# An all-engine loop moved half a stage earlier between the experts of a mixture, with new numbers for the ring of weights

## The chip, the cores and the metric

The kernel runs on one core of a Trainium2 chip. The metric is device time in microseconds (us). Before the change the median of three runs is 1884.03 us (1882.94 to 1884.06).

## The reference, cut to what matters

Two layers work on 512 tokens of width 1024 in float32. Each layer mixes tokens (attention and a convolution side by side, merged by two gates), then sends every token to 2 of 32 experts, then adds gated embeddings:

```python
for i in range(DEPTH):                                   # DEPTH = 2
    ...                                                  # h = norm(x); y_a: attention, y_b: convolution
    merged = sigmoid(ga) * y_a + sigmoid(gb) * y_b
    x = x + merged @ w_out[i]
    x = x + hier_moe(rms_norm(x), ...)                   # 32 experts, top 2
    g_ple = sigmoid(rms_norm(x) @ w_ple_gate[i])
    x = x + g_ple * (p[i] @ w_ple_proj[i])

hb = silu(xb @ w_gate[e]) * (xb @ w_up[e])               # one expert on its tokens
yb = hb @ w_down[e]
```

Every expert has its gate, up and down weights, 2 MB each, and all of them are read from memory once per layer. An expert that gets more tokens than a fixed capacity (64) must still serve them all.

## The kernel before, in words

**Mixing.** TensorE multiplies in three passes with numbers split in a high and a low half: each chunk of weights (a `raw` buffer of 512 KB, loaded at L207) is turned into `hi` by ScalarE (ACT, L225) and `lo` by GpSimd (POOL, L230); `s_hi` is read by the matmuls of L289 and L290, `s_lo` by those of L291. After the gates comes the merge, a loop over eight column blocks j = 0..7 with one chunk each (`ao0` to `ao7`). Block j has 12 matmuls into `ps_yb` and 12 into `ps_ya`. Then ScalarE adds a bias (L735), VectorE (DVE) applies the gates and adds (L736 to L738), and two halves of the result are split again: ScalarE writes `s_mTh` (L741), VectorE `s_mTl` (L742). The output product (`wo`) and the routing follow.

**Experts.** The 32 experts are 16 pairs, two pairs at a time: eight double pairs, c = 0..7. A double pair c runs gate and up products for both pairs (`ps_g`, `ps_u`, twice 32 matmuls each), then the third (down) products of double pair c - 1 (`ps_y`, 64 matmuls), transposes (`ps_hT`), the gather of the tokens for c + 1 (`ps_xg`) and the combination of double pair c - 1 into the tokens (`ps_c`). At c = 5 and 6 the embeddings' products (`ps_pe`) stand at the end; what they need is loaded at the start of c = 4 by `load_embeddings`: one tile `pT` (L1110), split by ScalarE and GpSimd, and two chunks at L207.

**Weights.** A double pair uses 48 pieces of 512 KB, 8 for each gate, up or down matrix of a pair. SyncE's queue (SP) issues them in the order of use, at L241 in `pump`, into `s4`, a pool of 45 buffers that serves many other tiles too. `pump(limit, keep)` stops when `limit` pieces are held, or when fewer than `keep` buffers would stay free. `RING` holds the limits in the mixing, one for each of three stretches; `KEEP` the reserved buffers for each c. After the routing's last steps `pump(keep=3)` is called with its default limit, 99; the last four pieces of double pair 0 come in halves (L253).

**The loop.** `overflow(l)` (L1218, L1219) handles crowded experts: a loop over as many extra blocks as the routing found. Its count is known only on the chip. With these inputs it is zero in both layers: no instruction of its body is in the trace. It is bracketed by barriers on which every engine waits, for all the others and for all transfers issued ahead of it. Before the change it stands behind the combination of c = `OVC` = 4.

**What sets the order.** The order on TensorE is the order of the code. On the other engines a scheduler sets it from the code and its own estimates. SP holds 8 transfers in flight; a piece's issue waits for the one 8 places ahead and for its buffer.

Of the kernel before, what the change touches and what calls it, by code (L numbers as in the profile page):

```python
# [53 lines left out]
              + [f"wo{i}" for i in range(8)] + ["pe0", "pe1"] + [f"pg{i}" for i in range(8)])  # L54
NCH = len(SEQ_CHUNKS)

RING = 6, 18, 28
KEEP = 6, 10, 6, 6, 8, 10, 12, 8
LAGS = 1, 2, 1, 5
OVC = 4  # L60
PEC = 5
PGD = "pg1", "pg2", "pg3"
PGS = 1, 3, 4, 5, 7
# [92 lines left out]
class Trunk:  # L156
# [310 lines left out]
    def mixer(self, l):  # L467
# [256 lines left out]
        for j in range(8):  # L724
# [20 lines left out]
            self.s4.free()  # L745
            self.pump(RING[0] + j)
        for s in oT + tuple(cv):
            s.free()
        self.pump(RING[1])


        pacc = [self.ps.get(F32, "wo") for _ in range(NT)]
        for i in range(4):
            self.step_b(pos[f"wo{i}"], pacc, mT, 2 * i, i == 0, i == 3)
            self.pump(RING[1])
        for t in range(NT):
# [10 lines left out]
        def hook():  # L767
            self.advance(steps)
            self.pump(RING[2], keep=3)
        for t in range(NT):  # L770
# [194 lines left out]
    def moe(self, l):  # L965
# [6 lines left out]
        def make_rows():  # L972
            for q in self.slots + list(self.gates) + [self.rc]:
                ps = self.ps.get(F32, "row")
                for t in range(NT):
                    pe.transpose(ps[:, t * P:(t + 1) * P], q[:, t:t + 1].to_broadcast([P, P]), self.ident)
                r_ = self.s2.get(F32, "row")
                act.activation(r_, ps, AF.Copy)
                self.ps.free()
                rows.append(r_)  # L980
# [23 lines left out]
        def scatter_hot(p):  # L1004

            col = self.cc(C_SLOT + p, 1)
            tmp = self.s2.get(F32, "oh")
            ga = self.tn(3, "ga", bufs=2)
            g_, rh[p] = self.tn(1, f"gs{p % 2}", bufs=2), self.tn(1, f"rs{p % 2}", bufs=2)
            v.tensor_scalar(tmp, rows[0], col, None, op0=OP.is_equal)  # L1010
            o = self.s2.get(F32R, "OHT")
            v.scalar_tensor_tensor(o, rows[1], col, tmp, op0=OP.is_equal, op1=OP.add)
            v.scalar_tensor_tensor(tmp, o.bitcast(F32), 0.5, rows[4], op0=OP.mult, op1=OP.mult, accum_out=rh[p])
            for i in range(2):
                v.scalar_tensor_tensor(tmp, rows[i], col, rows[2 + i], op0=OP.is_equal, op1=OP.mult,
                                       accum_out=ga[:, i:i + 1])
            v.tensor_scalar(g_, ga[:, 0:1], ga[:, 1:2], 2.0, op0=OP.add, op1=OP.mult)
            v.tensor_scalar(g_, g_, rh[p], rh[p], op0=OP.mult, op1=OP.mult)
            oht[p], gs[p] = o, g_
            self.s2.free()  # L1020

        def gate_up(p, xg, w, ps, hs):
            for h in hs:
                for k in range(2):
                    for e in range(2):
                        s = (2 * h + k) % 4 * GS + (2 * p % 4 + e) * CAP
                        pe.matmul(ps[64 * e:64 * e + 64], xg[h // 2][:, s:s + CAP], self.half_item((l, w, 2 * p + e, h), k),
                                  start=h == 0 and k == 0, stop=h == 3 and k == 1)
                for e in range(2):
                    self.item_free((l, w, 2 * p + e, h))  # L1030
                self.pump(keep=KEEP[self.c])

        def hidden(p, pg, pu):
            t = self.s2.get(F32, "h")
            act.activation(t, pg, AF.Tanh, scale=rh[p])  # L1035
            v.scalar_tensor_tensor(t, t, 1.0, pg, op0=OP.add, op1=OP.mult)  # L1036
            v.tensor_mul(t, t, pu)
            self.ps.free(2)
            return t

        def transp(p, t):
            ps = self.ps.get(F32, "hT")
            for f in range(4):
                pe.transpose(ps[:, f * P:(f + 1) * P], t[:, f * P:(f + 1) * P], self.ident)
            o = self.s2.get(F32, "hT")
            act.activation(o, ps, AF.Copy)  # L1046
            self.ps.free()
            self.s2.free()
            hT[p] = o

        def down(p):
            h_ = hT.pop(p)
            ps = [self.ps.get(F32, "y") for _ in range(2)]
            for f in range(4):
                for n in range(2):
                    for e in range(2):
                        pe.matmul(ps[n][64 * e:64 * e + 64], h_[:, f * P + e * CAP:f * P + (e + 1) * CAP],
                                  self.item_tile[l, "d", 2 * p + e, f][:, n * T:(n + 1) * T], start=f == 0, stop=f == 3)
                for e in range(2):
                    self.item_free((l, "d", 2 * p + e, f))  # L1060
                self.pump(keep=KEEP[self.c])
            self.s2.free()
            yh, yl = self.s4.get(F32R, "yh"), self.s4.get(F32R, "yl")
            for n in range(2):
                a = slice(n * T, (n + 1) * T)
                self.last = act.activation(yh[:, a], ps[n], AF.Copy, scale=gs[p]).ins
                v.scalar_tensor_tensor(yl[:, a], ps[n], gs[p], yh[:, a].bitcast(F32), op0=OP.mult, op1=OP.subtract)
            self.ps.free(2)
            ys[p] = (yh, yl)

        def combine(pl, then=None):
            for t in range(NT):
                for n in range(2):
                    ps = self.ps.get(F32, "c")
                    for i, p in enumerate(pl):
                        for o in range(2):
                            pe.matmul(ps, oht[p][:, t * P:(t + 1) * P], ys[p][o][:, n * T:(n + 1) * T],
                                      start=i == 0 and o == 0, stop=i == len(pl) - 1 and o == 1)
                    xs = self.x[t][:, n * T:(n + 1) * T]
                    v.tensor_add(xs, xs, ps)  # L1080
                    self.ps.free()
                if t == NT - 1:
                    self.s4.free(2 * len(pl))
                    self.s2.free(len(pl))
                if then:
                    then(t)

        def restore():

            self.x = [self.s4.get(F32, "x") for _ in range(NT)]  # L1090
            for x_, hi, lo in zip(self.x, *self.nh):
                nc.gpsimd.tensor_tensor(x_, hi.bitcast(F32), lo.bitcast(F32), op=OP.add)
# [14 lines left out]
        def load_embeddings():  # L1107
            self.pT = Rows(self.s4, 2, F32R, "pTh"), Rows(self.s4, 2, F32R, "pTl")
            praw = self.s4.get(F32, "pT")
            nc.sync.dma_start(praw, self.dr["pT"][l])  # L1110
            act.activation(self.pT[0].t[0], praw, AF.Copy)
            nc.gpsimd.tensor_tensor(self.pT[1].t[0], praw, self.pT[0].t[0].bitcast(F32), op=OP.subtract)
            self.s4.free()
            self.lim = self.pos["pe1"]
            self.look = self.ahead = 1
            self.load_chunks(self.lim)
            self.pp = []
# [9 lines left out]
        for c in range(NC2):  # L1127
            self.c = c
            prs = 2 * c, 2 * c + 1
            if c == PEC - 1:  # L1130
                load_embeddings()
            if c < NC2 - 1:
                oh = self.onehots(c + 1)
            ts = []
            for p in prs:
                pg, pu = self.ps.get(F32, "g"), self.ps.get(F32, "u")
                gate_up(p, xg, "g", pg, range(4))
                gate_up(p, xg, "u", pu, range(4))
                if p == 0:
                    with self.tc.issue_after(self.last_v), self.tc.issue_after(self.last_a):  # L1140
                        self.route()
                        make_rows()
                scatter_hot(p)
                ts.append(hidden(p, pg, pu))
            self.s4.free(2)
            if c == 1:
                restore()
            if c:
                for p in prs:
                    down(p - 2)  # L1150
            for p, t in zip(prs, ts):
                transp(p, t)
            if c < NC2 - 1:
                xg = [self.s4.get(F32, "xg") for _ in range(2)]
                for h in range(4):
                    gather(oh, xg, h)
                self.s4.free()
                if c == NC2 - 2:
                    self.s4.free(2 * NT)
            if c:  # L1160
                combine((2 * c - 2, 2 * c - 1))
            if c == OVC:
                self.overflow(l)
            if c in (PEC, PEC + 1):
                embeddings(c - PEC)
        self.lim = self.pos["pg7"]
# [317 lines left out]
```

## Time and profile before

| | |
|---|---|
| median of three runs | 1884.03 us |
| the profiled execution, whole | 1876.28 us |
| its span | 1874.5 us |
| TensorE busy | 1790.9 us (96%) |
| VectorE, ScalarE, GpSimd busy | 49%, 30%, 20% |
| transfers of the weights' queue | 477.04 MB, 66.9% of 16 engines' span |
| mean granted clock of TensorE | 0.989 |

The profiled execution lies 7.75 us below the median of the runs. TensorE sets the time; a change counts by what it adds to or takes from the time between two of its instructions. Busy time alone does not show a loss: a matmul that waits for its weights inside the pipeline can count as busy, so the prediction goes by starts.

### The profile page before, as it was taken

To read this page: it belongs to the slowest core of one execution; us is meant where nothing else is said; L and a number is where in the kernel's file an instruction comes from. 1 tells how busy PE (TensorE), PEld (TensorE's weight loads), DVE (VectorE), ACT (ScalarE), POOL (GpSimd) and SP (SyncE) were. 2 spreads that over 40 slices of the span, in tenths; PEclk is the share of its full clock that TensorE was granted. 3 is DMA by queue.
4 is the path that set the end of the run, shared out by engine and by line. 5 is a ranking of instruction groups with operands and counts; after the bars stand their busy time and mean duration, and the time that the engine had idled before them with its cause. 6 is when DMAs were issued, how large, how long until landed. Compare 5 with 4: busy or idle time off the path is not lost.

```text
span 1874.5 us, 23312 instructions
## 1 busy us (share of the span) xinstructions
PE 1790.9 (96%) x8532; PEld 1104.1 (59%) x8532; DVE 913.6 (49%) x2165; ACT 562.4 (30%) x1071; POOL 378.1 (20%) x201
## 2 busy tenths in 40 slices
PE   5999999999999989999989999999999999899987
PEld 4777777754555245454777767777545553455356
DVE  5587855463442243223657777536524432343146
ACT  4355443321111012113534445343211111021045
POOL 3445332401000001001444443242010000010021
PEclk9999999999999999999999999999999999999999
DMA  5212136389999899997231112554899999999951
GB/s 221 83 64 68 56 92 242 119 311 391 387 409 409 346 370 401 410 408 315 96 114 62 56 57 68 179 192 152 324 389 390 409 389 364 370 409 409 409 227 45
DMA packets 133319, 478.59 MB, mean 255 GB/s; under 512 B 14800, under 2 KB 15312, under 8 KB 133200
## 3 DMA queue, kind: packets, MB, share of 16 engines
q1 hardware_dynamic: 133200, 477.04, 66.9%
q8 instruction: 70, 1.15, 0.2%
q14 instruction: 49, 0.40, 0.1%
HBM read 474.89 MB, written 2.10 MB: 254 GB/s over the span
## 4 chain that ended last, share of the span: by engine, by line
PE 74%; DMA 10%; DVE 7%; issue 5%; ACT 2%; POOL 1%; SPq 0%; DVEq 0%; POOLq 0%; ACTq 0%
PE ps_g L94 11%; PE ps_u L94 10%; PE ps_y L94 9%; PE ps_z L290 5%; PE ps_z L289 5%; PE ps_z L291 5%; PE ps_xg L94 5%; PE ps_c L94 5%; DMA s_w<-wdn 4%; DMA s_w<-wg 3%; DMA s_w<-wu 2%; PE ps_tb L289 2%; PE ps_tb L290 2%; PE ps_tb L291 2%; PE ps_S L609 2%
## 5 line engine op out<-in xcount | busy, mean ns | idle before, releaser
L230 POOL TENSOR_TENSOR s_lo<-s_raw,s_hi 128x1024 fp32r<-128x1024 f32 x114 | 272.4, 2400 | 915.8 <-ACT s_hi L225 610.7
L94 PE MATMUL ps_g<-s_w,s_xg 128*64 128x512 f32 x1024 | 229.9, 602 | 11.2 <-DMA s_w<-wg 11.2
L94 PE MATMUL ps_y<-s_w,s_hT 128*64 128x512 f32 x1024 | 236.1, 595 | 3.5 <-DMA s_w<-wdn 2.9
L94 PE MATMUL ps_u<-s_w,s_xg 128*64 128x512 f32 x1024 | 231.2, 593 | 5.1 <-DMA s_w<-wu 4.9
L290 PE MATMUL ps_z<-s_hTl,s_hi 128*128 128x512 f32 x512 | 203.8, 398 | 0.0
L289 PE MATMUL ps_z<-s_hTh,s_hi 128*128 128x512 f32 x512 | 201.3, 393 | 0.0
L291 PE MATMUL ps_z<-s_hTh,s_lo 128*128 128x512 f32 x512 | 199.7, 390 | 0.0
L94 PEld LDWEIGHTS ps_y<-s_w,s_hT 128*64 128x64 f32 x1024 | 75.4, 137 | 159.9 <-issue 130.8
L94 PEld LDWEIGHTS ps_u<-s_w,s_xg 128*64 128x64 f32 x1024 | 74.0, 137 | 157.2 <-issue 141.1
L94 PEld LDWEIGHTS ps_g<-s_w,s_xg 128*64 128x64 f32 x1024 | 72.7, 139 | 155.4 <-issue 150.3
L501 DVE SCALAR_TENSOR_TENSOR s_acc<-ps_z,smt,s_acc 128x511 f32<-128x511 f32 (+27 forms) x210 | 153.8, 732 | 4.2
L1080 DVE TENSOR_TENSOR s_x<-s_x,ps_c 128x512 f32<-128x512 f32 x128 | 86.9, 688 | 89.4 <-PE ps_c L94 60.0
L225 ACT ACTIVATE s_hi<-s_raw 128x1024 fp32r<-128x1024 f32 x120 | 125.9, 1058 | 8.8 <-DMA s_raw<-wd 4.5
L94 PE MATMUL ps_xg<-s_OH,s_xh 128*128 128x256 f32 x476 | 117.4, 288 | 3.8 <-DVE s_OH L950 1.9
L1035 ACT ACTIVATE s_h<-ps_g,rs 128x512 f32<-128x512 f32 x32 | 22.0, 689 | 319.3 <-PE ps_g L94 286.5
L1046 ACT ACTIVATE s_hT<-ps_hT 128x512 f32<-128x512 f32 x32 | 17.7, 598 | 328.1 <-PE ps_hT L94 287.1
L94 PE MATMUL ps_xg<-s_OH,s_xl 128*128 128x256 f32 x476 | 115.9, 285 | 0.0
L290 PEld LDWEIGHTS ps_z<-s_hTl,s_hi 128*128 128x128 f32 x512 | 96.3, 188 | 21.2 <-issue 3.0
L289 PEld LDWEIGHTS ps_z<-s_hTh,s_hi 128*128 128x128 f32 x512 | 96.1, 188 | 21.3 <-issue 1.0
L1036 DVE SCALAR_TENSOR_TENSOR s_h<-s_h,ps_g 128x512 f32<-128x512 f32 x32 | 22.0, 688 | 177.5 <-ACT s_h L1035 177.5
L291 PEld LDWEIGHTS ps_z<-s_hTh,s_lo 128*128 128x128 f32 x512 | 96.3, 188 | 18.9
L94 PEld LDWEIGHTS ps_xg<-s_OH,s_xh 128*128 128x128 f32 x476 | 92.2, 194 | 5.7 <-issue 5.7
(256 smaller groups left out, 2852.4 us busy)
## 6 DMA issues: line engine op xcount, KB each, us to landing
s_w<-wu SPq DMA_DIRECT2D x256, 512.0 KB, 10.2
s_w<-wdn SPq DMA_DIRECT2D x256, 512.0 KB, 10.2
s_w<-wg SPq DMA_DIRECT2D x248, 512.0 KB, 10.2
s_raw<-wd SPq DMA_DIRECT2D x124, 512.0 KB, 3.5
s_w<-wg SPq DMA_DIRECT2D x16, 256.0 KB, 7.5
s_x<-x SPq DMA_DIRECT2D x4, 512.0 KB, 9.7
out<-s_n SPq DMA_DIRECT2D x8, 256.0 KB, 2.0
s_gain<-gains SPq DMA_DIRECT2D x3, 512.0 KB, 3.6
```

Of the source, the lines that this page charges most:

```text
L94: i = f(*a, **k)
L225: nc.scalar.activation(hi, raw, AF.Copy)
L230: nc.gpsimd.tensor_tensor(lo, raw, hi.bitcast(F32), op=OP.subtract)
L289: mm(out, lh, rh, start=start, stop=False)
L290: mm(out, lh, rl, start=False, stop=False)
L291: mm(out, ll, rh, start=False, stop=stop)
L501: v.scalar_tensor_tensor(o, i, w, o, op0=OP.mult, op1=OP.add)
L609: nc.tensor.matmul(ps[:, off:off + n], qk(0, i * P, (i + 1) * P)[r], qk(1, 0, n)[r], start=True, stop=True)
L1035: act.activation(t, pg, AF.Tanh, scale=rh[p])
L1036: v.scalar_tensor_tensor(t, t, 1.0, pg, op0=OP.add, op1=OP.mult)
L1046: act.activation(o, ps, AF.Copy)
L1080: v.tensor_add(xs, xs, ps)
```

## The change

The loop moves from the end of double pair 4 to double pair 3, directly behind the third products, ahead of the transposes, the gather and the combination. The limits of the ring in the mixing rise, and fewer buffers are reserved in most double pairs.

```diff
-RING = 6, 18, 28
-KEEP = 6, 10, 6, 6, 8, 10, 12, 8
+RING = 10, 21, 34
+KEEP = 2, 5, 5, 9, 5, 5, 5, 2
 LAGS = 1, 2, 1, 5
-OVC = 4
+OVC = 3
...
             if c:
                 for p in prs:
                     down(p - 2)
+            if c == OVC:
+                self.overflow(l)
             for p, t in zip(prs, ts):
                 transp(p, t)
...
             if c:
                 combine((2 * c - 2, 2 * c - 1))
-            if c == OVC:
-                self.overflow(l)
```

On TensorE in layer 0 the loop's instructions stand, before, behind the last combination of double pair 4 and ahead of the first gate product of double pair 5 (`s_OHT` is the table that scatters results back to tokens):

```order
L94 MATMUL ps_c_5204<-s_yl_5029,s_OHT_4498 128x512
L94 MATMUL ps_c_5204<-s_yh_5064,s_OHT_4580 128x512
L94 MATMUL ps_c_5204<-s_yl_5065,s_OHT_4580 128x512
L1218 TENSOR_LOAD nov
L1219 COMPARE_AND_BRANCH
L1219 UNCONDITIONAL_BRANCH x2
```

After the change, behind the last third product of double pair 3:

```order
L94 MATMUL ps_y_4630<-s_w_4543,s_hT_4284 64x512
L94 MATMUL ps_y_4630<-s_w_4549,s_hT_4284 64x512
L1218 TENSOR_LOAD nov
L1219 COMPARE_AND_BRANCH
L1219 UNCONDITIONAL_BRANCH x2
```

The transposes `ps_hT`, the gather `ps_xg` and the combination `ps_c` of double pair 3 now stand behind the loop.

On SP before, in layer 0, the loop has 238 issues of L241 ahead of it, the last two of them gate pieces (`s_w` from `wg`):

```order
L241 DMA s_w_5052<-wu 128x1024
L241 DMA s_w_5054<-wu 128x1024
L241 DMA s_w_5060<-wg 128x1024
L241 DMA s_w_5062<-wg 128x1024
L1219 COMPARE_AND_BRANCH
L1219 UNCONDITIONAL_BRANCH x2
```

After the change 193, the last five of them gate pieces, and the embeddings' loads come directly behind the loop:

```order
L241 DMA s_w_4639<-wu 128x1024
L241 DMA s_w_4641<-wg 128x1024
L241 DMA s_w_4647<-wg 128x1024
L241 DMA s_w_4649<-wg 128x1024
L241 DMA s_w_4655<-wg 128x1024
L241 DMA s_w_4657<-wg 128x1024
L1219 COMPARE_AND_BRANCH
L1219 UNCONDITIONAL_BRANCH x2
L1110 DMA s_pT_5053<-pT 128x1024
L207 DMA s_raw_5057<-wd 128x1024
L207 DMA s_raw_5059<-wd 128x1024
L241 DMA s_w_5084<-wg 128x1024
```

The loop stands 45 pieces earlier in SP's list. In both versions 34 issues of L241 stand ahead of those of L253, at the start of the experts.

On ScalarE in the merge of layer 0, before, the split of the chunk for block 4 (`s_hi_2362`) stands ahead of the two halves of block 3's result (`s_mTh`, from `ps_ya_2368`):

```order
L735 ACTIVATE ps_yb_2369<-ps_yb_2369,smt 128x512
L225 ACTIVATE s_hi_2362<-s_raw_2206 128x1024
L741 ACTIVATE s_mTh_2234<-ps_ya_2368 128x256
L225 ACTIVATE s_hi_2404<-s_raw_2324 128x1024
L741 ACTIVATE s_mTh_2236<-ps_ya_2368 128x256
L735 ACTIVATE ps_yb_2411<-ps_yb_2411,smt 128x512
```

After the change the same split (`s_hi_2370`) stands behind both halves (from `ps_ya_2376`):

```order
L735 ACTIVATE ps_yb_2377<-ps_yb_2377,smt 128x512
L741 ACTIVATE s_mTh_2234<-ps_ya_2376 128x256
L741 ACTIVATE s_mTh_2236<-ps_ya_2376 128x256
L225 ACTIVATE s_hi_2370<-s_raw_2206 128x1024
L225 ACTIVATE s_hi_2412<-s_raw_2332 128x1024
L735 ACTIVATE ps_yb_2419<-ps_yb_2419,smt 128x512
```

Each ScalarE instruction starts behind the one above it, so the split of block 4's weights now comes behind work on block 3's finished sums. The same exchange is there in layer 1.

## Rows read from the trace of the kernel before

**Rows 1.** Chain that ended last, layer 0: start, us, what
```profile
551.35 7.02 PE ps_g L94 x32
...
578.97 13.73 PE ps_y L94 x64
...
608.67 7.02 PE ps_g L94 x32
...
744.91 5.44 PE ps_pe L94 x24
750.35 7.02 PE ps_g L94 x32
```

**Rows 2.** Chain that ended last, layer 1
```profile
1505.32 13.73 PE ps_y L94 x64
...
1676.39 7.02 PE ps_g L94 x32
```

**Rows 3.** TensorE's timeline at the loop, layers 0 and 1: start, us, line [idle before <-releaser]
```profile
683.84 8.60 PE L94 MATMUL ps_g<-s_w,s_xg 128*64 128x512 f32 x32 [5.57 <-DMA s_w<-wg]
...
1610.71 9.37 PE L94 MATMUL ps_g<-s_w,s_xg 128*64 128x512 f32 x32 [5.65 <-DMA s_w<-wg]
```

**Rows 4.** Chain that ended last, around the loop, layer 0
```profile
673.16 10.09 DMA s_w<-wg
...
683.27 0.03 SPq L1219
```

**Rows 5.** SP's queue, layer 0
```profile
598.94 9.26 SPq L241 DMA_DIRECT2D s_w<-wg  x8
609.14 0.33 SPq L1110 DMA_DIRECT2D s_pT<-pT  x1
...
623.73 4.99 SPq L241 DMA_DIRECT2D s_w<-wu  x8
630.51 19.96 SPq L241 DMA_DIRECT2D s_w<-wdn  x16
651.43 9.29 SPq L241 DMA_DIRECT2D s_w<-wg  x8
661.67 9.25 SPq L241 DMA_DIRECT2D s_w<-wu  x8
671.89 14.80 SPq L241 DMA_DIRECT2D s_w<-wg  x8
```

**Rows 6.** SP's queue, layer 1
```profile
1525.30 9.30 SPq L241 DMA_DIRECT2D s_w<-wg  x8
```

**Rows 7.** Windows: us, busy us of each engine, granted clock, DMA share, GB/s
```profile
392.00:394.00 2.00, 0.30 (x2) 0.33 (x3) 1.97 (x18) 0.00 (x0) 0.00 (x0) 1.00 1.05 382
684.00:686.00 2.00, 2.00 (x6) 0.60 (x8) 2.00 (x5) 0.00 (x0) 0.00 (x0) 0.50 0.55 127
```

**Rows 8.** ScalarE's timeline in the merge, layer 0
```profile
297.16 0.39 ACT L741 ACTIVATE s_mTh<-ps_ya 128x256 fp32r<-128x256 f32 x1 [0.49 <-DVE s_mTl L742]
...
298.19 1.05 ACT L225 ACTIVATE s_hi<-s_raw 128x1024 fp32r<-128x1024 f32 x1
301.72 0.39 ACT L741 ACTIVATE s_mTh<-ps_ya 128x256 fp32r<-128x256 f32 x1 [2.48 <-DVE ps_ya L738]
```

**Rows 9.** VectorE's and GpSimd's timelines there
```profile
302.14 0.42 DVE L742 SCALAR_TENSOR_TENSOR s_mTl<-ps_ya,s_mTh 128x256 fp32r<-128x256 f32 x1 [0.45 <-ACT s_mTh L741]
...
299.31 2.38 POOL L230 TENSOR_TENSOR s_lo<-s_raw,s_hi 128x1024 fp32r<-128x1024 f32 x1 [22.24 <-ACT s_hi L225]
```

**Rows 10.** TensorE's timeline there, layers 0 and 1
```profile
300.06 0.39 PE L289 MATMUL ps_yb<-s_cv,s_hi 128*128 128x512 f32 x1
...
300.74 0.39 PE L290 MATMUL ps_ya<-s_oTl,s_hi 128*128 128x512 f32 x1
301.75 0.50 PE L291 MATMUL ps_yb<-s_cv,s_lo 128*128 128x512 f32 x1 [0.62 <-POOL s_lo L230]
...
1227.74 0.50 PE L291 MATMUL ps_yb<-s_cv,s_lo 128*128 128x512 f32 x1 [0.62 <-POOL s_lo L230]
```

## The prediction, made before the changed kernel ran

> **What bounds the kernel now.** I read the chain of waits first, then TensorE's timeline where that chain leaves TensorE, then SP's queue, and last the merge of the mixing stage on four engines. The reader is to see a double pair's plain price. Double pair 3 runs from its first gate product at 551.35 to that of double pair 4 at 608.67: 57.32 us, with TensorE on the chain [rows 1]. Double pairs 4 and 5 together should cost twice that and one set of embedding products, 2 x 57.32 + 5.44 = 120.08 us. They take 750.35 - 608.67 = 141.68 [rows 1]. So 21.60 us are lost there in layer 0. In layer 1 the third products of double pair 3 end at 1505.32 + 13.73 = 1519.05 and double pair 6 starts at 1676.39, 157.34 us later [rows 2]. In layer 0 the way from their end (578.97 + 13.73 = 592.70) to double pair 4 is 15.97 us, so the plain price is 136.05 and the loss 21.29.
>
> The loss has two sources. At the loop TensorE stands still for 5.57 and 5.65 us and then needs 8.60 and 9.37 us for 32 matmuls that elsewhere take 7.02 [rows 1, 3]; the granted clock is 0.50 in the first window, the lower of its two levels [rows 7]. The stop ends with transfers: the piece that lands at 673.16 + 10.09 = 683.25 releases SP's loop instruction at 683.27 [rows 4], and TensorE starts at 683.84, 0.59 us after that landing. The rest of the loss is weights that come too late in double pair 4. SP issues a run of 8 gate pieces at 598.94 and the tile `pT` 10.20 us later, so a piece takes 1.28 us of the shared transfers. After `pT`, at 609.14, the next pieces follow only at 623.73 [rows 5]: the queue held back for 14.6 us, and TensorE then caught up with it.
>
> **The loop, new place.** It is a wait for every transfer issued ahead of it, so its price is the landing of the last of them against TensorE's arrival. Arrival: 592.70. The last piece ahead is number 193 of SP's list. The loop stood behind number 238, second of the run issued at 671.89; counting back over runs of 8, 8, 16 and 8, the run at 598.94 holds 189 to 196, so 193 is its fifth [rows 5]. It goes out at 598.94 + 4 x 1.28 = 604.1 and lands 10.2 later (the 10.09 of [rows 4] and its issue), at 614.3. Adding 0.6 gives a restart at 614.9: a stop of 22.2 us. Layer 1: the run starts at 1525.30 [rows 6], the piece lands at 1540.6, the restart is 1541.2, the stop 22.2. I assume that pieces are issued no earlier than before: in this stretch the runs follow each other at 1.28 us a piece, so that transfers, not buffers, set the pace, and other reserves don't speed it up.
>
> What this buys: the 21.60 and 21.29 us go, if double pairs 4 and 5 then run at their plain price. At the loop 193 issued pieces and the 4 loaded in halves count 197; used are 28 + 3 x 48 = 172 of the list and those 4. That leaves 21 pieces on the chip when TensorE restarts, and 15.97 us of work (transposes, gather, combination) that needs no weights. Double pair 4 would start at 614.9 + 15.97 = 630.9, double pair 6 at 751.0 instead of 750.35: +0.6 us, layer 1 +0.9. The loads of the embeddings, which held the queue for 14.6 us, now fall where 21 pieces lie ready. New pieces then follow every 1.28 us from about 635 on (an estimate: restart of use at 630.9, a free buffer, and some 3 us for a transfer on an empty queue). Number 268, the last that double pair 5 multiplies, lands at 635 + 74 x 1.28 = 729.7; TensorE wants it at 630.9 + 57.3 + 41.4 = 729.6 (41.4 is 592.70 - 551.35). That is the narrowest place, with no reserve: I count nothing for it and keep 3 us a layer as an upper bound.
>
> The cold start moves and does not go: before, the loss of 21.6 contained 8.60 - 7.02 = 1.58 us (layer 1: 2.35) for it, now it comes on top of the 22.2 [rows 1, 3]. The work that it slows is another (transposes and gather), so bounds are 0 and 3 us; I take the same 1.6 and 2.35. The Trainium skill speaks against this change here: "TensorE: Matmul & The Clock Gate", section "Loop structure matters more than you think", has TensorE fall to the lower clock over a long wait for a transfer. The trace agrees, with 0.50 behind 5.57 us, and by page and row alike each layer still has one such wait, now four times as long.
>
> Sum for the experts: 0.6 + 1.6 = 2.2 and 0.9 + 2.35 = 3.25, together **+5.5 us** (bounds: 1.5 without the cold start, 13.5 with 3 us for it and 3 us for late weights in both layers).
>
> **The merge.** Raising RING adds no instruction, but it shifts SP's issues, and the scheduler then places one ScalarE instruction elsewhere. Before, the split of block 4's chunk runs at 298.19, well ahead of its first use at 300.06 [rows 8, 10]. Afterwards it is queued behind both L741 of block 3. The first can't start before block 3's sums exist, 301.72 [rows 8]. The second waits for VectorE's L742 [rows 8], which ends at 302.14 + 0.42 = 302.56 [rows 9]; it takes 0.39. So the split starts at 303.0 and ends at 304.0, and TensorE's first product of block 4 starts at about 304.1 instead of 300.06: 4.0 us late. GpSimd's low half follows with 2.38 us [rows 9], at 306.5, and the third product (L291) starts at 306.6. It now stands behind two products, not four, as the code orders block 4 in 12 and 12; 22 products are left where before, at 301.75 [rows 10], 20 were left. With 0.23 us from start to start (300.06 and 300.74 lie three steps apart) block 4 ends at 306.6 + 22 x 0.23 = 311.6 against 301.75 + 20 x 0.23 = 306.35. That is **+5.3 us** a layer; the same wait for GpSimd in layer 1 is there at 1227.74 [rows 10], so twice: +10.6. Who waits for TensorE then: blocks 5 to 7 and the whole output product, a chain without reserve that ends in the experts' start. Only the later split of block 5's chunk gains, since TensorE comes later too.
>
> Bounds of this term: nothing, if ScalarE's order did not decide (I see no way, since an engine takes its instructions in their order), or -1 a layer, if a later short wait for GpSimd vanishes in the delay; and 7.7 a layer, if the stop lowers the clock and 2.35 come on top. A stop of about 1.7 us at 392 to 394 leaves the granted clock at 1.00 [rows 7], one of 5.6 lowers it; 4.0 and then 2.0 lie between, nearer to the short one each, so I add none. By the page named above a wait that is long enough costs the lower clock; with it the sum would be 3.2 to 4.7 us more, and no row settles it.
>
> **Ring and reserves elsewhere.** At the start of the experts both versions hold 34 pieces, since the last call of `pump` in the mixing has the same default limit; the new RING loads them earlier, where TensorE multiplies from `s_hi` and `s_lo` and does not wait for them. Cost nothing, hidden by those products; if a `raw` chunk comes later for it, the price is the wait of one chunk, 1.28 us a piece ahead of it, at most a few us, kept in the range.
>
> Sum: 5.5 + 10.6 = **+16.1 us**. The profiled execution was 1876.28 (its span 1874.5); the new one comes to 1892.4. The median lay 7.75 above the profiled one, so I add to the median: 1884.03 + 16.1 = **1900 us**.
>
> **Rivals.**
> *Transfers already landed (faster).* If piece 193 is in before TensorE arrives, the loop costs about 2 us with a warm clock, the 21.6 and 21.3 go, and the kernel gains some 39 us on the experts and pays 10.6 in the merge: about 1856. A weaker form with other reserves that let SP run 12 us ahead gives 1876. It decides from a landing before 592.7. The skill's "Perfetto Trace Analysis", section "Optimization Strategy", reads repeated gaps as too few buffers; lowered reserves would then mend them. Against it: the gaps are in double pairs 4 and 5 alone, the runs follow at the transfers' pace, and 193 lands 21.6 us after that arrival [rows 5].
> *The merge costs nothing.* The change then shows the experts alone, +1.5 to +5.5: 1885.5 to 1889.5. For it: the instruction is 1.05 us long. Against it: TensorE needs its result at 300.06, and it can't start before 303.0.
> *Late weights behind the stop.* SP's queue stands idle from 614.3 until TensorE uses pieces again, less the three loads of the embeddings; with no reserve at number 268, 3 us more a layer in double pair 5, and the colder start in gather and merge: 1904 to 1913.
>
> **How the numbers follow.** The forecast (1892 to 1904) gets 0.58, late weights 0.16, a free merge 0.16, landed transfers 0.10. A measurement of this kernel can tell 0.2%, 3.8 us, from no change, so "same" is 1880.3 to 1887.8. Faster: 0.10, the last rival. Same: the lower half of the free merge, and a remainder of mixed cases, 0.13. Slower: 0.77. The range for 8 in 10 reaches down to 1884 and up to 1911.
>
> **What would show it.** Right: TensorE idle for about 22 us ahead of `ps_hT` in double pair 3 in both layers, released by a gate piece; no stop ahead of double pair 5; double pairs 4 and 5 near 120 us together; in the merge both L741 ahead of L225 and TensorE late by 4 us at block 4, then waiting 2 us for `s_lo`. Wrong: a stop at the loop of under 12 us (pieces landed sooner), a late double pair 5 (weights), or block 4 on time.

## The result: slower by 1.5%, outside the range

The changed kernel takes 1911.84 us (median of four runs, 1910.15 to 1912.65) against 1883.49 before (four runs): a ratio of 1.0151, 95% interval 1.0133 to 1.0168, 28.35 us more. The direction was forecast, the size was not: 1900 was said, with a range up to 1911.

The profiled execution has a span of 1910.9 us, 36.4 more than the one shown of before. Part of that is not the change: in five of the experiments below, which touch nothing there, the first stretch of the attention takes 1.6 us longer than in the profiled execution of before, and in most of them the last stage 1.5 us. So the terms below are taken stage by stage, each from its own start.

TensorE's timeline of the changed kernel at the loop, layers 0 and 1 (start, us, line, and in brackets the idle time before it and what ended it):

```profile
589.91 13.90 PE L94 MATMUL ps_y<-s_w,s_hT 128*64 128x512 f32 x64
...
626.17 1.97 PE L94 MATMUL ps_hT<-c,s_h 128*128 128x128 f32 x8 [22.36 <-DMA s_w<-wg]
...
643.98 7.09 PE L94 MATMUL ps_g<-s_w,s_xg 128*64 128x512 f32 x32
...
701.30 7.09 PE L94 MATMUL ps_g<-s_w,s_xg 128*64 128x512 f32 x32
...
1568.91 1.97 PE L94 MATMUL ps_hT<-c,s_h 128*128 128x128 f32 x8 [22.69 <-DMA s_w<-wg]
```

The stop ahead of the transposes is 22.36 and 22.69 us, released by a gate piece; 22.2 was forecast. The stop ahead of double pair 5 [rows 3] is gone, and double pair 4 runs at its plain price: 701.30 - 643.98 = 57.32 us, as double pair 3 before [rows 1].

SP's queue behind it:

```profile
610.29 5.44 SPq L241 DMA_DIRECT2D s_w<-wg  x5
625.85 0.33 SPq L1110 DMA_DIRECT2D s_pT<-pT  x1
626.23 0.90 SPq L207 DMA_DIRECT2D s_raw<-wd  x2
641.10 3.10 SPq L241 DMA_DIRECT2D s_w<-wg  x3
644.25 6.08 SPq L241 DMA_DIRECT2D s_w<-wu  x8
```

Five gate pieces go out ahead of the loop. Behind it the three loads of the embeddings go at once, and then nothing until 641.10, just before TensorE uses weights again. The bill for this comes in double pair 5, in TensorE's timeline:

```profile
738.81 2.35 PE L94 MATMUL ps_y<-s_w,s_hT 128*64 128x512 f32 x8 [0.21 <-DMA s_w<-wdn]
741.38 2.34 PE L94 MATMUL ps_y<-s_w,s_hT 128*64 128x512 f32 x8 [0.22 <-DMA s_w<-wdn]
743.93 1.93 PE L94 MATMUL ps_y<-s_w,s_hT 128*64 128x512 f32 x6 [0.21 <-DMA s_w<-wdn]
```

Eight matmuls start every 2.56 us, twice the 1.28 us of a transfer, where 64 of them took 13.73 us when weights lay ready [rows 1], 1.72 for eight. The idle times shown are only 0.2 us each; the lateness is in the spacing of the starts. Double pair 5 is 65.9 us long where 62.76 is plain (57.32 and one set of embedding products, 5.44). The chain that ended last shows the piece that decides it, number 268, the last that double pair 5 multiplies. It lands at 733.71 + 10.18 = 743.89, and TensorE goes on at once:

```profile
733.71 10.18 DMA s_w<-wdn
743.93 1.93 PE ps_y L94 x6
```

The merge, on ScalarE and then on TensorE:

```profile
303.44 0.38 ACT L741 ACTIVATE s_mTh<-ps_ya 128x256 fp32r<-128x256 f32 x1 [3.46 <-DVE ps_ya L738]
304.32 0.38 ACT L741 ACTIVATE s_mTh<-ps_ya 128x256 fp32r<-128x256 f32 x1 [0.49 <-DVE s_mTl L742]
304.60 2.00 ACT L225 ACTIVATE s_hi<-s_raw 128x1024 fp32r<-128x1024 f32 x2
```

```profile
305.70 0.64 PE L289 MATMUL ps_yb<-s_cv,s_hi 128*128 128x512 f32 x1 [3.76 <-ACT s_hi L225]
306.14 0.63 PE L290 MATMUL ps_yb<-s_cv,s_hi 128*128 128x512 f32 x1
308.14 0.79 PE L291 MATMUL ps_yb<-s_cv,s_lo 128*128 128x512 f32 x1 [1.37 <-POOL s_lo L230]
308.73 0.63 PE L289 MATMUL ps_yb<-s_cv,s_hi 128*128 128x512 f32 x1
309.15 0.63 PE L290 MATMUL ps_yb<-s_cv,s_hi 128*128 128x512 f32 x1
...
312.57 0.47 PE L289 MATMUL ps_ya<-s_oTh,s_hi 128*128 128x512 f32 x1
```

Order and waits are as forecast: the split behind both halves, 3.76 us for it, then a wait for GpSimd. What was not counted is in the starts: ten steps from 308.14 to 312.57 take 4.43 us instead of 10 x 0.23. The windows of that stretch (us, busy us of PE, PEld, DVE, ACT and POOL, granted clock, DMA share, GB/s) name the cause, a granted clock of 0.50, the lower level:

```profile
305.50:306.00 0.50, 0.30 (x1) 0.30 (x2) 0.00 (x0) 0.50 (x2) 0.28 (x1) 0.90 0.00 0
306.00:308.00 2.00, 0.76 (x2) 0.04 (x1) 0.00 (x0) 0.59 (x1) 2.00 (x1) 0.50 0.00 0
308.00:310.00 2.00, 1.86 (x4) 1.49 (x5) 0.00 (x0) 0.00 (x0) 2.00 (x2) 0.50 0.42 82
310.00:312.00 2.00, 2.00 (x6) 1.60 (x5) 0.00 (x0) 0.00 (x0) 0.41 (x1) 0.50 0.55 188
312.00:314.00 2.00, 2.00 (x8) 1.58 (x8) 0.50 (x1) 0.66 (x1) 0.00 (x0) 0.82 0.00 0
```

The clock fell at 305.9 (a mean of 0.90 from 305.5 to 306.0, 0.50 from then on), 0.2 us behind the end of the first wait and ahead of the second, and rose at 312.7. The two products between the waits start 0.44 us apart already.

The kernel before has something like it in the routing of layer 1: two shorter waits, 0.2 us apart, and a granted clock of 0.50 from 1318.4 on, so a mean of 0.60 and then 0.55 over two windows:

```profile
1316.64 0.18 PE L891 MATMUL ps_pos<-Mb,trib 128*128 128x32 bf16 x1 [1.68 <-DVE Mb L876]
1318.69 0.55 PE L94 MATMUL ps_xg<-s_OH,s_xh 128*128 128x256 f32 x1 [1.88 <-DVE s_lgw L914]
```

```profile
1318.00:1320.00 2.00, 1.31 (x6) 1.34 (x7) 1.00 (x10) 0.50 (x2) 0.00 (x0) 0.60 1.03 378
1320.00:1322.00 2.00, 2.00 (x12) 2.00 (x12) 0.00 (x0) 1.99 (x5) 0.00 (x0) 0.55 0.37 139
```

From the merge's first product into `ps_ya` to the output product's first it is 50.3 us against 43.1 before (layer 1: 49.8 against 43.0).

### The profile page after: what moved, and what is told of

Its sections match the earlier page's. It is cut to its first block, busy times and chain, and to the rows that moved or that the text cites. A ratio compares the mean times of both kernels' runs of the same rounds, so it can differ in the third digit from the quotient of the medians.

```text
span 1910.9 us, 23332 instructions
## 1 busy us (share of the span) xinstructions
PE 1789.5 (94%) x8532; PEld 1114.5 (58%) x8532; DVE 911.8 (48%) x2165; ACT 562.8 (29%) x1071; POOL 378.4 (20%) x201
## 4 chain that ended last, share of the span: by engine, by line
PE 70%; DMA 15%; DVE 7%; issue 5%; ACT 2%; POOL 1%; SPq 0%; DVEq 0%; POOLq 0%; ACTq 0%
PE ps_g L94 9%; PE ps_u L94 9%; PE ps_y L94 7%; DMA s_w<-wdn 6%; PE ps_xg L94 6%; PE ps_z L290 5%; PE ps_z L289 5%; PE ps_z L291 5%; PE ps_c L94 5%; DMA s_w<-wg 4%; DMA s_w<-wu 4%; PE ps_tb L289 2%; PE ps_tb L290 2%; PE ps_tb L291 2%; PE ps_S L609 2%
## 5 line engine op out<-in xcount | busy, mean ns | idle before, releaser
L94 PE MATMUL ps_y<-s_w,s_hT 128*64 128x512 f32 x1024 | 227.9, 593 | 1.3 <-DMA s_w<-wdn 1.3
L94 PE MATMUL ps_u<-s_w,s_xg 128*64 128x512 f32 x1024 | 225.2, 592 | 0.0
L291 PE MATMUL ps_z<-s_hTh,s_lo 128*128 128x512 f32 x512 | 200.5, 392 | 0.0
L94 PE MATMUL ps_xg<-s_OH,s_xh 128*128 128x256 f32 x476 | 122.6, 296 | 3.8 <-DVE s_OH L950 3.8
L94 PE MATMUL ps_xg<-s_OH,s_xl 128*128 128x256 f32 x476 | 120.8, 292 | 0.0
L289 PEld LDWEIGHTS ps_z<-s_hTh,s_hi 128*128 128x128 f32 x512 | 96.5, 189 | 21.6 <-issue 1.0
L291 PEld LDWEIGHTS ps_z<-s_hTh,s_lo 128*128 128x128 f32 x512 | 96.6, 189 | 19.1
L94 PEld LDWEIGHTS ps_xg<-s_OH,s_xh 128*128 128x128 f32 x476 | 96.3, 202 | 7.6 <-issue 7.6
```

Of the source, the lines that this page charges most:

```text
L94: i = f(*a, **k)
L289: mm(out, lh, rh, start=start, stop=False)
L291: mm(out, ll, rh, start=False, stop=stop)
```

## Experiments

Each was timed beside the kernel before on the same chip; "c = 0 to 6" is the time from the first gate product of double pair 0 to that of double pair 6 in layer 0, from the starts on TensorE. It is 353.1 us before and 358.8 in the changed kernel. The kernel before took 1881.09 us beside e1 to e4, 1882.07 beside e5 to e8 and 1882.53 beside e9 to e12, so a difference between experiments of different groups is uncertain by about 1 us more.

### e1: the first number of RING alone

```diff
-RING = 6, 18, 28
+RING = 10, 18, 28
```

> The kernel before with the first number of RING alone raised from 6 to 10; loop and reserves as before. Theory A (the merge's delay and the lower clock behind it are paid by the first number of RING, apart from the loop): in both layers the split of block 4's chunk stands behind block 3's two halves, TensorE stops about 3.8 and 1.4 us there, the granted clock is 0.50 for some 5 us behind it; 7 us a layer in the merge and 1 to 2 in the routing, so 13 to 18 us slower than before: 1896 to 1902. Rival B (the merge's delay is absorbed before the experts start, and the loop carries the whole difference): within 4 us of before.

Measured: 1895.5 against 1881.09 us, ratio 1.0069 (1.0055 to 1.0084), 14.4 us more. TensorE's timeline in the merge:

```profile
306.02 0.57 PE L289 MATMUL ps_yb<-s_cv,s_hi 128*128 128x512 f32 x1 [3.75 <-ACT s_hi L225]
...
308.45 0.80 PE L291 MATMUL ps_yb<-s_cv,s_lo 128*128 128x512 f32 x1 [1.44 <-POOL s_lo L230]
```

The same two waits, with the loop at its old place; c = 0 to 6 is 353.4, as before. Theory A holds, B falls: one limit in the mixing costs 14.4 us. The merge takes 50.3 and 50.0 us, 14.2 more than before for both layers together, so nearly all of it is there, by the order that the scheduler gives ScalarE and the clock behind the wait. The 1 to 2 us a layer that A added for the routing did not come.

### e2: the changed kernel with that number put back

```diff
-RING = 10, 21, 34
+RING = 6, 21, 34
```

> The changed kernel with the first number of RING put back to 6 (6, 21, 34). Theory A: the merge is as before (block 4 starts without the 3.8 us stop), the loop's part stays: 11 to 15 us slower than before, 1894 to 1899. Rival B: as the changed kernel, 1910 or more.

Measured: 1896.48, ratio 1.0075 (1.0062 to 1.0088), 15.4 us more than before. The merge takes 43.1 us again, c = 0 to 6 takes 359.9. With e1 that is 14.4 + 15.4 = 29.8, against the 28.35 of the whole change: the two parts add up, and the rest of RING costs nothing that shows.

### e3: the loop alone

```diff
-KEEP = 6, 10, 6, 6, 8, 10, 12, 8
-OVC = 4
+KEEP = 6, 10, 6, 9, 8, 10, 12, 8
+OVC = 3
...                      (the loop's two lines moved as in the change)
```

> The kernel before with the loop at its new place alone; RING as before, KEEP as before but for 9 in double pair 3, which the loop's own buffers need. Theory A (the stop is the landing of the last piece issued ahead, and the late weights in double pair 5 come from the queue that stands idle behind the loop, whatever the reserves): the stop is 22 to 23 us in both layers and the time within 5 us of the kernel with RING 6, 21, 34. Rival C (the lowered reserves make the late weights or lengthen the stop): at least 5 us faster than that one.

Measured: 1896.51, ratio 1.0076 (1.0063 to 1.0089), the same as e2 to 0.03 us; stops of 22.43 and 22.25 us. The lowered reserves and the two later numbers of RING neither cost nor give anything with the loop at this place; rival C falls. The loop's place alone is 15.4 us.

### e4: the loop behind the last double pair

```diff
-OVC = 4
+OVC = 7
```

> The kernel before with the loop behind the combination of the last double pair (OVC = 7), where all 380 pieces of SP's list are issued ahead of it and no piece follows. Theory A (the price is the last landing against TensorE's arrival, plus the pieces that are held up behind): the loss of 5.6 us of stop, 1.6 to 2.4 of lower clock and the late weights behind it goes, the new stop is under 5 us, since the last pieces are in by then: 6 to 16 us faster than before, 1868 to 1878. Rival D (each passage of the loop costs its stop and cold start wherever it stands): within 4 us of before.

Measured: 1890.37, ratio 1.0042 (1.0030 to 1.0054): 9.3 us slower, a miss of mine on both counts. TensorE at the new place and SP's queue there:

```profile
871.49 16.27 PE L94 MATMUL ps_y<-s_w,s_hT 128*64 128x512 f32 x64 [6.39 <-DMA s_w<-wdn]
```

```profile
821.01 39.95 SPq L241 DMA_DIRECT2D s_w<-wdn  x32
871.17 3.87 SPq L207 DMA_DIRECT2D s_raw<-wd  x8
```

c = 0 to 6 falls to 349.6, so 3.5 us are won there. But the last 32 pieces go out until 861, and the last lands at 871. Without the loop TensorE uses those one by one as they land. With it, it waits for all of them, 6.39 us, and then runs 64 matmuls in 16.27 us instead of the 13.9 of a warm start. The way from double pair 7 to the next stage is 77.6 us instead of 69.8.

### e5: fewer pieces ahead of the loop

On the kernel of e2; 187 pieces stand ahead of the loop.

```diff
-KEEP = 2, 5, 5, 9, 5, 5, 5, 2
+KEEP = 2, 5, 5, 15, 5, 5, 5, 2
```

> The changed kernel with RING 6, 21, 34 and 15 instead of 9 buffers reserved in double pair 3: 187 instead of 193 pieces stand ahead of the loop. Both theories: the last piece lands 6 x 1.28 = 7.7 us sooner, so the stop falls from 22.4 to about 15 us. Theory F (in the second half of the experts the transfers are the bound, and the time is set by how long SP's queue stands idle): what the stop gives is taken back by late weights in double pairs 4 to 6, so within 4 us of the kernel with RING 6, 21, 34. Rival G (the stop on TensorE is itself the price): 2 x 7.7 less, 12 to 16 us faster than that kernel.

Measured: 1880.95, ratio 0.9991 (0.9980 to 1.0003): 15.5 us faster than e2 and no different from before. The stops are 15.61 and 14.37 us, 6.8 and 7.9 less than in e2: a piece ahead of the loop lengthens the stop by close to its 1.28 us, as forecast. And what the stop gave was not taken back: Theory F's forecast, which I held, fell here, and G's came true. SP's queue shows why:

```profile
591.74 8.02 SPq L241 DMA_DIRECT2D s_w<-wu  x7
610.20 0.33 SPq L1110 DMA_DIRECT2D s_pT<-pT  x1
610.57 0.90 SPq L207 DMA_DIRECT2D s_raw<-wd  x2
611.52 0.43 SPq L241 DMA_DIRECT2D s_w<-wu  x1
611.99 16.57 SPq L241 DMA_DIRECT2D s_w<-wg  x8
```

Of the six buffers left free ahead of the loop, five take pieces right behind it, by 614.0, while TensorE transposes and gathers, which needs no weights; the sixth piece goes out at 621.2. The reserve moves pieces from ahead of the stop to behind it and leaves the queue idle for less time. That is F's own premise, the idle queue: what failed is the expectation that a larger reserve would leave the idle time as long as it was (the table at e9 to e12 has it).

### e6: the kernel of e2 without the loop

```diff
-            if c == OVC:
-                self.overflow(l)
```

> The changed kernel with RING 6, 21, 34 and without the loop; it leaves out the serving of crowded experts, which these inputs do not need. Theory F: the stop goes, but the pieces behind the embeddings' loads are late again as in the kernel before, since SP holds the next chunk for the split of the embeddings' tile: 18 to 30 us faster than with the loop there, 1866 to 1878. Rival G: the stop and the cold start go whole, 46 us or more faster, 1850 or less.

Measured: 1867.65, ratio 0.9922 (0.9910 to 0.9935): 28.8 us faster than e2, as F forecast. c = 0 to 6 is 346.2 and not the plain 331.4 that the double pairs' prices would give (39.4 + 4 x 57.3 + 62.8): double pair 4 takes 67.9 us again, with matmuls spaced by the transfers, as before the change. Ahead of double pair 6, e4 has no loop either and takes 349.6, and 348.6 against 346.4 in layer 1; it differs in KEEP and in RING. So these numbers do count where no stop hides them; which of them it is, no run separates.

### e7: the kernel before, with SP's hold removed

The raw tile `pT` is split into its halves late in double pair 4, so the chunks behind it get other buffers and need not wait for the split.

```diff
         def load_embeddings():
-            self.pT = Rows(self.s4, 2, F32R, "pTh"), Rows(self.s4, 2, F32R, "pTl")
-            praw = self.s4.get(F32, "pT")
+            self.praw = praw = self.s4.get(F32, "pT")
             nc.sync.dma_start(praw, self.dr["pT"][l])
-            act.activation(self.pT[0].t[0], praw, AF.Copy)
-            nc.gpsimd.tensor_tensor(self.pT[1].t[0], praw, self.pT[0].t[0].bitcast(F32), op=OP.subtract)
-            self.s4.free()
...
+        def split_embeddings():
...
                 for p in prs:
                     down(p - 2)
+            if c == PEC - 1:
+                split_embeddings()
```

> The kernel before with the split of the embeddings' tile issued late in double pair 4 instead of at its start, so that the chunks and the pieces behind them get other buffers and SP's queue is not held for the split. The loop stays behind double pair 4's combination. Theory F: some 10 us of idle queue go in each layer; TensorE reaches the loop sooner and stops there longer (about 11 us instead of 5.6), and 6 to 8 us a layer are won: 1865 to 1870. Rival H (the hold cost nothing, weights were late for another reason): within 4 us of before.

Measured: 1868.15, ratio 0.9923 (0.9910 to 0.9936): 13.9 us faster than before, inside the forecast. SP's queue and TensorE behind the loop:

```profile
612.29 0.33 SPq L1109 DMA_DIRECT2D s_pT<-pT  x1
613.57 1.62 SPq L207 DMA_DIRECT2D s_raw<-wd  x2
616.14 9.28 SPq L241 DMA_DIRECT2D s_w<-wu  x8
```

```profile
680.38 9.37 PE L94 MATMUL ps_g<-s_w,s_xg 128*64 128x512 f32 x32 [6.72 <-DMA s_w<-wg]
```

The pieces follow `pT` after 3.9 us instead of 14.6 [rows 5]. So the hold was worth 7 us a layer, and rival H falls. The stop at the loop grew to 6.72 us and not to the 11 that I expected, since double pair 4 still waits for weights: c = 0 to 6 is 346.2.

### e8: the same late split on the kernel of e2

```diff
...                      (as in e7)
```

> The changed kernel with RING 6, 21, 34 and the same late split of the embeddings' tile. Theory F: the idle queue behind the loop has another cause, the free buffers, which come back only when TensorE uses pieces again; so little is won, at most 4 us. Rival H': the loads of the embeddings hold the queue there too, and 10 us or more are won.

Measured: 1891.09, ratio 1.0045 (1.0033 to 1.0057): 5.4 us faster than e2, more than F's 4, which is a miss, and far from the 10 of H'. Double pair 5 takes 64.2 us instead of 66.2. Behind the loop at its new place most of the idle queue is free buffers that are missing; a smaller part is the hold.

### e9 to e12: how far this goes

On the kernel of e5: e9 has 24 reserved buffers (178 pieces ahead of the loop); e10 has 18 (184) and the late split of e7; e11 has 24 and the late split; e12 is e11 with another first number of RING.

```diff
-KEEP = 2, 5, 5, 15, 5, 5, 5, 2
+KEEP = 2, 5, 5, 24, 5, 5, 5, 2        (e9, e11, e12; e10: 18)
-RING = 6, 21, 34
+RING = 5, 21, 34                      (e12 alone)
```

> As the run with 15 reserved buffers, with 24: 178 pieces ahead of the loop instead of 193. The stop should fall by 15 x 1.28 = 19.2 us to about 3. Theory G (the stop is the price, and the reserved buffers let the queue go on at once behind the loop): 9 x 1.28 x 2 = 23 us faster than with 15, 1856 to 1862. Theory F' (too few pieces lie ready behind the loop, so weights come late in double pairs 4 to 6): half of that or less is won, 1866 to 1876.

> The changed kernel with RING 6, 21, 34, 18 reserved buffers in double pair 3 (184 pieces ahead of the loop) and the late split of the embeddings' tile. Stop about 22.4 - 9 x 1.28 = 10.9 us. Theory G: 1864 to 1870. Theory F': 1870 to 1878.

> As the run before, with 24 reserved buffers: 178 pieces ahead of the loop, stop about 3 us. Theory G: 1850 to 1858, faster than both kernels of the study. Theory F': 1860 to 1870.

> As the run with 24 reserved buffers and the late split, with 5 as the first number of RING: both splits of the chunks for blocks 4 and 5 then stand ahead of block 3's halves on ScalarE. If the merge's time follows ScalarE's order, the wait of 0.6 us for GpSimd at block 4 or the one of 1.0 at a later block shrinks: 1 to 3 us faster than with 6. If the order costs something else, no difference beyond 2 us.

| kernel | us | ratio to before (95%) | stop, layer 0 | c = 0 to 6, layer 0 | transfers idle, layer 0 |
|---|---|---|---|---|---|
| e9 | 1868.27 | 0.9919 (0.9905 to 0.9933) | 3.25 | 345.7 | 5.2 |
| e10 | 1868.06 | 0.9921 (0.9909 to 0.9934) | 10.88 | 345.6 | 5.2 |
| e11 | 1868.13 | 0.9922 (0.9909 to 0.9935) | 2.90 | 345.1 | 4.9 |
| e12 | 1868.78 | 0.9928 (0.9916 to 0.9940) | 3.10 | 345.3 | 4.9 |
| e6 | 1867.65 | 0.9922 (0.9910 to 0.9935) | none | 346.2 | 6.0 |
| e7 | 1868.15 | 0.9923 (0.9910 to 0.9936) | 6.72 | 346.2 | 5.6 |
| e4 | 1890.37 | 1.0042 (1.0030 to 1.0054) | 6.39, at c = 7 | 349.6 | 9.0 |
| e5 | 1880.95 | 0.9991 (0.9980 to 1.0003) | 15.61 | 351.5 | 10.8 |
| before | | | 5.57 | 353.1 | 12.9 |
| e1 | 1895.50 | 1.0069 (1.0055 to 1.0084) | 5.89 | 353.4 | 13.1 |
| e8 | 1891.09 | 1.0045 (1.0033 to 1.0057) | 22.53 | 357.0 | 16.5 |
| e3 | 1896.51 | 1.0076 (1.0063 to 1.0089) | 22.43 | 358.1 | 17.6 |
| changed | 1911.84 | 1.0151 (1.0133 to 1.0168) | 22.36 | 358.8 | 18.4 |
| e2 | 1896.48 | 1.0075 (1.0062 to 1.0088) | 22.40 | 359.9 | 19.4 |

The stops came out as forecast (3, 10.9, 3 us). The times did not follow them: e9 and e11 miss G and meet F', e10 meets G, and with e6 and e7 six kernels end within 1.2 us of each other, though their stops are none, 3, 7 and 11 us. TensorE in double pairs 4 and 5 of e11 shows what they wait for, then the chain there and the window over both:

```profile
655.18 2.34 PE L94 MATMUL ps_y<-s_w,s_hT 128*64 128x512 f32 x8 [0.21 <-DMA s_w<-wdn]
657.74 2.35 PE L94 MATMUL ps_y<-s_w,s_hT 128*64 128x512 f32 x8 [0.22 <-DMA s_w<-wdn]
...
719.45 2.35 PE L94 MATMUL ps_y<-s_w,s_hT 128*64 128x512 f32 x8 [0.22 <-DMA s_w<-wdn]
```

```profile
711.63 10.34 DMA s_w<-wdn
722.01 1.93 PE ps_y L94 x6
```

```profile
600.00:720.00 120.00, 118.00 (x571) 55.28 (x570) 38.58 (x85) 13.75 (x28) 2.40 (x1) 1.00 1.02 405
```

Behind the stop the transfers run at 405 GB/s without a pause, and the third products wait for each piece. A double pair needs 48 x 1.28 = 61.4 us of transfers and 57.3 of TensorE, so it eats 4 us of its lead each time; once the lead is gone, a shorter stop only lets TensorE wait elsewhere.

The last column puts a number on it. It is the time from the landing of piece 178 to that of piece 268 in the trace, less 1.28 us for each of the 93 transfers between (90 pieces and the three loads of the embeddings). In all fourteen kernels and both layers piece 178 lands 197.5 to 198.4 us behind the first gate product of double pair 0, and double pair 6 starts 23.3 us behind the landing of 268. So c = 0 to 6 is 198.0 + 93 x 1.28 + 23.3 = 340.3 us and the idle time of the transfers, within 0.5 us. That decides between F and G. At this place the stop is not the price: transfers still run while TensorE waits in it, and the 10.9 us of e10 cost no more than the 2.9 of e11. The price is the time in which no transfer runs, F's premise. With 9 reserved buffers it is 19.4 us (e2), with 15 it is 10.8 (e5), and with 24, or without the loop or the hold, some 5 to 6 us are left. That the six kernels leave so nearly the same idle time, by different causes, no run explains. Without any, c = 0 to 6 would still be 340.3 by this sum, and not the plain 331.4.

In e12 the wait for GpSimd at block 4 did not shrink but grew (1.08 us, in e11 0.63), and the time is the same within its spread; that order gives nothing.

All six are about 0.8% faster than the kernel before and, by their medians, 2.3% faster than the changed one. All keep the loop that serves crowded experts, apart from e6; e7 is the smallest edit, e9 the smallest that keeps the loop where the change put it.

## Why the prediction was wrong, point by point

- **The stop at the new place** was right: 22.2 us from the fifth piece of a run, 22.36 and 22.69 measured, and e5, e9 and e10 confirm the rule behind it, 1.28 us for each piece that stands ahead of the loop.
- **The loss of 21.6 and 21.3 us goes**: right for double pair 4 (57.32), wrong for double pair 5. The failing step is the sentence on number 268, "I count nothing for it and keep 3 us a layer as an upper bound". Double pair 5 took 3.1 us more than its plain price in the changed kernel (3.5 in layer 1) and 3.4 in e2. I had found a reserve of nothing at that place and then priced it at its lower end. The landing was too early: double pair 3 starts 11.1 us later in the changed kernel, so on the prediction's clock 268 landed at 732.8 and not at 729.7. Number 194 came about when forecast, at 633.7, but the 74 steps behind it took 99.1 us instead of 94.7, the first of them 3.4. The time at which TensorE wants the piece, 729.6, was right by luck: it is the end of the third products, 1.9 us after the piece is needed (the 1.93 of the chain above), and it leaves out the cold start of 1.9. Put by the sum behind the table above: for plain double pairs 4 and 5 the transfers could have stood idle for 353.1 + 0.6 + 1.6 - 340.3 = 15.0 us; they did for 18.4. The rival *Late weights behind the stop* named this mechanism and its price and got 0.16; it was the case that came, with the merge's clock beside it.
- **The cold start**: 1.97 us for eight transposes that took 1.02 to 1.09, and a gather of 8.62 instead of 7.67, 1.9 together (1.6 in layer 1); the 1.6 and 2.35 taken from other work fit.
- **The merge, order and waits**: right to 0.3 us (3.76 for the split). The order on TensorE is not always that of the code: before, two products into `ps_ya` stand ahead of block 4's first L291 [rows 10], after the change none does. The prediction counted that.
- **The merge, clock**: the second failing step. "4.0 and then 2.0 lie between, nearer to the short one each, so I add none." The first wait was enough. In both layers of the changed kernel and of e1 the clock fell to 0.50 near its end, from 0.8 us ahead of it to 0.3 behind, and each time ahead of the second wait. Ten steps took 4.43 us instead of 2.3, so 2.1 us a layer; the merge cost 7.2 and 6.8 instead of 5.3. A row of the kernel before spoke against the guess: in its layer 1, as shown above, two waits of 1.68 and 1.88 us close together were enough for 0.50; the single wait of [rows 7] was the mild case. The Trainium skill's page "TensorE: Matmul & The Clock Gate", section "Loop structure matters more than you think", has TensorE go cold over a long wait for a transfer; the trace shows the same, 0.50 behind 3.76 us, for a wait on ScalarE. The "3.2 to 4.7 us more" that the prediction named and left out was the better sum: 4.2 came.
- **The routing**, a term I did not have, is not shown to belong to the change: 52.0 and 51.8 us from the routing's first transposes to the first gate product, against 50.3 and 50.7. But e5, e8 and e10, whose merge is that of before, have 51.7 to 51.9 in both layers, and e1, whose merge is the changed one, has 50.8 in both. A stretch of the lower clock, which lies at 383 to 390 us before and at 401 to 408, in the gather, in the changed kernel, may be the reason; no run isolates it.
- **Ring and reserves elsewhere** at nothing: right for this change (e2, e3).

In sum the loop's part was put at +5.5 us and measured at +15.4 (e2, e3), the merge's at +10.6 and measured at +14.4 (e1); their upper bounds were 13.5 and 15.4. In the profiled execution of e2, 13.0 us of the loop's part lie between double pairs 0 and 6 (359.9 against 353.1 in layer 0, 358.9 against 352.7 in layer 1), 7.5 more than forecast. The late weights of double pair 5 are 6.7 of that (66.2 and 66.0 us against 62.76), a stop and cold start of 25.0 instead of 23.8 in layer 0 another 1.2, and layer 1's came 0.3 under the forecast. Where the other 2.4 us of the 15.4 lie stays open: the routing and the stages behind double pair 6 differ by up to 1.8 us each between kernels that are alike there.

## What to carry to other kernels

A wait for all transfers lasts until the landing of the last one issued ahead of it, so its length is set by how many pieces stand ahead in the queue. Its price is another matter. Check whether the transfers bind soon after: here they did, and only the time in which none ran counted, whatever the stop. So hold pieces back ahead of such a wait, and there are buffers to fill right behind it, while work that needs no transfers runs. Several edits that each look good alone can remove the same idle time and end at the same place. And a change of a limit in one stage can reorder another engine's instructions: read the scheduled order of every engine, then price a stall with the clock that it leaves behind.

## What the runs showed that I had not expected

Three numbers. A stall of 3.76 us was enough for a granted clock of 0.50, from 0.2 us behind its end until 312.7, before a second stall of 1.37 had begun. Late weights show in the trace as idle times of 0.2 us only, while eight matmuls need 2.56 us instead of 1.72. And six kernels with stops from none to 11 us ended between 1867.65 and 1868.78 us, while in all fourteen the way to double pair 6 was 340.3 us and the idle time of the transfers, within 0.5 us.
